# Forgetting attention in a hybrid encoder layer: one PSUM bank moved from the transposed scores to the side products

## The chip, the cores and the metric

The kernel runs on one core of a Trainium2 chip. Five engines work from queues of their own: TensorE (PE; its weight loads are PEld), VectorE (DVE), ScalarE (ACT), GpSimd (POOL) and SyncE (SP), which here issues the transfers. The metric is the device time of one execution in microseconds; lower is better. All times of the trace are microseconds from the start of its span.

## What is computed

One layer of a streaming encoder on 1024 tokens of width 1024, in float32: `h = x + W_out [FoX ++ GLA]`, then cross attention to 256 memory tokens, then a squared-ReLU MLP. The part that matters is the forgetting attention (FoX) with 8 heads of width 64, and the memory's keys and values, which do not depend on it:

```python
# forgetting attention, per head; c = cumulative sum of the log forget gates
s = einsum('bqhd,bkhd->bhqk', qb, kb) * scale
s = where(k_pos <= q_pos, s + c[q] - c[k], -inf)
out = einsum('bhqk,bkhd->bqhd', softmax(s), vb)
# memory side of the cross attention
k, v = split(rms_norm(mem) @ wkv, 2)
k = rms_norm(k)
# output projection of both mixers
h = x + concat([fox_out, gla_out]) @ w_out
```

## The kernel before

Matmul operands are split into a high and a low part (fp32r), and `gemm` (lines 103 to 110) makes three matmuls for each 128 rows of the sum: high x high, low x high, high x low. `evac_split` (112) takes a finished PSUM tile out in two instructions: ACT copies it (the high part), then DVE subtracts that copy from the tile (the low part). A PSUM tile of 128 x 512 floats is called a bank here.

`mixer_inputs` makes the projections, the gated linear attention (GLA) and, at its end, the values of FoX. It opens FoX (`fox_open`, 593) and starts the first group of scores before the values are done.

`fox` (646) loops over 8 heads and, in each head, over 2 groups. `fox_group` makes the scores of four blocks of 128 queries. `fox_scores` (617) does each: matmuls of queries and keys (628, 629) and a mask (631) into a score tile, the negated maximum on DVE (633), the exponential with its sum on ACT (636), the reciprocal on DVE (638), and the scaling on POOL (639). `values` (655) then takes two query blocks: for each pair of key blocks it transposes the probabilities on PE (666, 668) into a bank `tr`, takes it out with `evac_split` (671), and multiplies with the values into `pv` (675, 676). Line 678 (ACT) and line 681 (DVE) take `pv` out into `mixf`. A head has four calls of `values`, with 1, 2, 3 and 4 such `tr` tiles: 80 in all.

After each call of `values`, `step` (688) runs a piece of `side_work` (705), which is meant to lie beside the attention. It consists of the GLA half of the output projection for the first 512 columns (`out_part`, 758, 8 products of 12 matmuls), the keys and values of the memory (731 to 754, 8 products of 24 matmuls), and the second 512 columns with the GLA half and the first four FoX heads (8 products of 18 matmuls). Each product fills one bank `mm`. `out_part` takes it out with one DVE addition (776), the memory's keys with an ACT copy (744), its values with `evac_split` (738). The keys are also transposed, through a bank of `tr` (749 to 752), into a tile `mkv` that exists once and is emptied by a store (753).

The PSUM pools while FoX runs:

| pool | tiles | banks |
|---|---|---|
| `mm2` (651) | `mm`, the side products | 1 |
| `pv2` (652) | `pv` | 1 |
| `tr2` (653) | `tr`, transposed scores and memory keys | 3 |
| `sps` (596) | `s1` (one bank), `s2` (two banks), the scores | 3 |

That makes eight. After FoX, the next projection (`project_out`, 808) opens `mm3` with 2 banks, `tr3` with 2 (225, 226) and `mm3b` with 4 (812). It adds the rest of the FoX heads: its first operands are splits of `mixf` (`split_half`, 794), one for each pair of heads.

The order of the instructions on each engine is not written by hand. The Tile framework plans it at build time (`schedule_with_timeline_sim=True`, 1311) from the program order and its own estimate of each duration: an instruction takes its place when its operands and its buffer are free by that estimate. On the chip each engine runs its queue in that fixed order, and waits where an operand or a buffer is late. A pool that lands on the bytes of closed pools waits for every user of them, unless it is opened with `reuse_waits="tile"`, which these are not.

Of the kernel before, what the change touches and what calls it, by code (L numbers as in the profile page):

```python
# [24 lines left out]
PSUM = bass.MemoryType.PSUM  # L25
# [22 lines left out]
def f(ap):  # L48
    return ap.bitcast(F32)


class Layer:
# [593 lines left out]
    def fox(self):  # L646
        nc = self.nc
        with ExitStack() as st:
            pt = self.open(st, "foxpt", 5)
            olp = self.open(st, "foxol", 3)  # L650
            mmp = self.open(st, "mm2", 1, space=PSUM)
            pvp = self.open(st, "pv2", 1, space=PSUM)
            trp = self.open(st, "tr2", 3, space=PSUM)

            def values(h, sb, pp, A):
                va = A[4]
                pv = self.T(pvp, [P, 256], F32, "pv")
                nb = 2 * sb + 2
                for b in range(sb + 1):
                    tp = self.T(trp, [P, 512], F32, "tr")  # L660
                    for j in range(2):
                        kb = 2 * b + j
                        for i in range(2):
                            o = tp[:, j * 256 + i * P:j * 256 + (i + 1) * P]
                            if kb > 2 * sb + i:
                                nc.tensor.matmul(o, self.zerob, self.zerob, start=True, stop=True)
                            else:
                                nc.tensor.transpose(o, pp[i][:, kb * P:(kb + 1) * P], self.ident)  # L668
                    th = self.T(pt, [P, 512], F32R, "pth")
                    tl = self.T(pt, [P, 512], F32R, "ptl")  # L670
                    self.evac_split(th, tl, tp)
                    for j in range(2):
                        kb = 2 * b + j
                        js = slice(j * 256, (j + 1) * 256)
                        nc.tensor.matmul(pv, va[:, kb, :], th[:, js], start=kb == 0, stop=False)  # L675
                        nc.tensor.matmul(pv, va[:, kb, :], tl[:, js], start=False, stop=kb == nb - 1)  # L676
                ol = self.T(olp, [64, 256], F32, "ol")
                nc.scalar.activation(ol, pv[64:128, :], AF.Copy)
                o = self.mixf[(h % 2) * 64:(h % 2) * 64 + 64, 2 * sb:2 * sb + 2, h // 2, :]
                v3 = lambda ap: ap.rearrange("p (a b) -> p a b", a=2)  # L680
                nc.vector.tensor_tensor(o, v3(pv[0:64, :]), v3(ol), ALU.add)

            side = self.side_work(self.side, mmp, trp)
            prep = self.fox_prep
            next(side)
            A = self.fox_first

            def step(s):
                for _ in range(((s + 1) * 30 + 8) // 32 - (s * 30 + 8) // 32):
                    next(side, None)  # L690

            for h in range(8):
                nc.sync.dma_start(f(A[4]), self.vd[:, h])
                for g in range(2):
                    pp = self.fox_group(h, g, A) if h + g else self.fox_p
                    if g == 0 and h < 7:
                        An = prep(h + 1)
                    for sb in (g, g + 2):
                        values(h, sb, (pp[2 * sb], pp[2 * sb + 1]), A)
                        step(4 * h + 2 * g + sb // 2)  # L700
                A = An
            for _ in side:
                pass
# [611 lines left out]
```

## Time and profile before

| | |
|---|---|
| median of 3 runs | 1467.38 us (1467.37 to 1469.64) |
| the profiled execution as a whole | 1473.37 us |
| its span, first to last instruction | 1471.6 us |
| mean granted TensorE clock | 0.989 |
| FoX with side work, after the values' projection | 335 to 577 us of the span |

A row of the view by stretch gives the stretch, its length, and for each engine the busy time with the number of instructions, then the granted TensorE clock as a share of full speed, the busy share of the DMA engines and GB/s. A row of the view of waits gives the engine and line that stood idle, what released it, the total, the number of times and the longest. A row of the timeline gives start, duration, engine, line, operation, the tiles written and read, the shape, how many equal instructions are merged, and in square brackets an idle time just before with its releaser. Matmuls are pipelined: the duration of one is longer than the distance to the next.

### The profile page before, as it was taken

How to read it: one execution, taken by the hardware profiler on the slowest of the kernel's cores; microseconds unless marked ns; L12 is line 12 of the kernel's file. 1: busy time of each engine (PE TensorE's matmuls, PEld its weight loads, DVE VectorE, ACT ScalarE, POOL GpSimd, SP SyncE). 2: the span in 40 equal slices, each digit the busy share in tenths (PEclk: the TensorE clock that was granted, in tenths of full speed). 3: DMA queues.
4: the chain of work that ended last, by engine and by line, in shares of the span. 5: the costliest groups of instructions: out<-in, count | busy, mean ns of one | idle time of the engine just before them, and what ended most of it. 6: DMA issues, size and time to landing. Idle time of an engine off the chain costs nothing.

```text
span 1471.6 us, 19266 instructions
## 1 busy us (share of the span) xinstructions
PE 1435.6 (98%) x7068; PEld 1198.2 (81%) x7068; DVE 934.8 (64%) x1328; ACT 685.1 (47%) x1095; POOL 431.7 (29%) x456
## 2 busy tenths in 40 slices
PE   9999999999998999999999999999999999999998
PEld 7777888887877787888888878887888878888887
DVE  5387412427776676656654885645556958788797
ACT  4464322326776555445442254545445736334230
POOL 4146503324473311621212200000000532333454
PEclk9999999999999999999999999999999999999999
DMA  7425620268576742414375124444445846337353
GB/s 273 124 47 129 153 74 4 72 159 266 181 205 197 194 156 70 144 38 136 115 243 214 44 72 172 172 172 162 169 160 212 313 132 210 126 110 231 108 205 122
DMA packets 121166, 223.94 MB, mean 152 GB/s; under 512 B 8912, under 2 KB 54512, under 8 KB 118512
## 3 DMA queue, kind: packets, MB, share of 16 engines
q1 hardware_dynamic: 119776, 218.25, 45.9%
q10 hardware_dynamic: 1296, 4.46, 1.0%
q8 instruction: 56, 0.92, 0.3%
q14 instruction: 38, 0.31, 0.1%
HBM read 150.59 MB, written 72.09 MB: 151 GB/s over the span
## 4 chain that ended last, share of the span: by engine, by line
PE 82%; DMA 7%; DVE 4%; ACT 3%; issue 2%; POOL 1%; SPq 0%; DVEq 0%; ACTq 0%
PE mm L108 14%; PE mm L109 14%; PE mm L110 13%; PE my L109 7%; PE my L110 7%; PE my L108 7%; PE tr L109 3%; PE tr L108 3%; PE tr L110 3%; PE tr L668 2%; DMA xt<-in_x_dram 1%; DMA raw<-in_w_in_dram 1%; PE pv L675 1%; PE pv L676 1%; PE s L628 1%
## 5 line engine op out<-in xcount | busy, mean ns | idle before, releaser
L108 PE MATMUL my<-x,g 128*128 128x512 f32 x464 | 180.8, 390 | 1.5 <-ACT h L1251 1.5
L109 PE MATMUL my<-x,g 128*128 128x512 f32 x464 | 180.9, 390 | 1.3 <-DVE x L1046 1.3
L110 PE MATMUL my<-x,g 128*128 128x512 f32 x464 | 180.7, 390 | 0.0
L108 PE MATMUL mm<-wh,xh 128*128 128x512 f32 x320 | 128.7, 403 | 0.3 <-ACT wh L97 0.3
L109 PE MATMUL mm<-wl,xh 128*128 128x512 f32 x320 | 127.7, 399 | 0.0
L110 PE MATMUL mm<-wh,xl 128*128 128x512 f32 x320 | 127.4, 398 | 0.0
L1045 ACT ACTIVATE g<-s 128x1024 fp32r<-128x1024 f32 (+1 forms) x72 | 68.9, 963 | 103.9 <-PE my L110 37.6
L1046 DVE TENSOR_TENSOR g<-raw,g 128x512 fp32r<-128x512 f32 (+3 forms) x72 | 67.9, 946 | 69.2 <-ACT g L1045 69.1
L1071 POOL TENSOR_TENSOR s<-raw 128x384 f32<-128x384 f32 (+1 forms) x20 | 25.6, 1279 | 282.9 <-issue 217.0
L108 PEld LDWEIGHTS my<-x,g 128*128 128x128 f32 x464 | 87.2, 188 | 19.9 <-ACT h L1251 1.9
L109 PEld LDWEIGHTS my<-x,g 128*128 128x128 f32 x464 | 87.2, 188 | 19.6 <-DVE x L1046 1.7
L1045 ACT ACTIVATE g<-raw 128x512 fp32r<-128x512 f32 (+3 forms) x72 | 55.5, 773 | 101.8 <-DMA raw<-in_mlp_w_dram 39.9
L110 PEld LDWEIGHTS my<-x,g 128*128 128x128 f32 x464 | 87.2, 188 | 18.0
L1046 DVE TENSOR_TENSOR g<-s,g 128x1024 fp32r<-128x1024 f32 (+1 forms) x72 | 88.7, 1236 | 7.2 <-ACT g L1045 7.2
L639 POOL TENSOR_SCALAR p<-p,rrec 128x128 f32<-128x128 f32 (+3 forms) x64 | 50.6, 792 | 126.6 <-DVE rrec L638 117.0
L1213 DVE TENSOR_TENSOR x<-x 128x1024 fp32r<-128x1024 f32 (+1 forms) x64 | 77.1, 1226 | 15.7 <-ACT x L1212 15.7
L108 PE MATMUL mm<-x,g 128*128 128x512 f32 x220 | 85.9, 390 | 0.0
L110 PE MATMUL mm<-x,g 128*128 128x512 f32 x220 | 85.8, 390 | 0.0
L109 PE MATMUL mm<-x,g 128*128 128x512 f32 x220 | 85.7, 390 | 0.0
L108 PE MATMUL tr<-x,g 128*128 128x512 f32 x212 | 82.6, 389 | 0.0
L110 PE MATMUL tr<-x,g 128*128 128x512 f32 x212 | 82.6, 389 | 0.0
L109 PE MATMUL tr<-x,g 128*128 128x512 f32 x212 | 82.6, 389 | 0.0
(319 smaller groups left out, 3787.3 us busy)
## 6 DMA issues: line engine op xcount, KB each, us to landing
ud<-h SPq DMA_DIRECT2D x32, 768.0 KB
x<-ud SPq DMA_DIRECT2D x48, 512.0 KB
raw<-in_mlp_w_dram SPq DMA_DIRECT2D x20, 1024.0 KB
raw<-in_mlp_w_dram SPq DMA_DIRECT2D x16, 768.0 KB
raw<-in_w_in_dram SPq DMA_DIRECT2D x23, 512.0 KB
raw<-in_xattn_wkv_dram SPq DMA_DIRECT2D x16, 512.0 KB
od<-o SPq DMA_DIRECT2D x32, 256.0 KB
ud<-h SPq DMA_DIRECT2D x32, 256.0 KB
```

What stands on the lines that cost most here:

```text
L108: mm(ps, lh[k], rh[k], start=start and k == 0, stop=False, **kw)
L109: mm(ps, lh[k], rl[k], start=False, stop=False, **kw)
L110: mm(ps, ll[k], rh[k], start=False, stop=stop and k == n - 1, **kw)
L628: nc.tensor.matmul(ps[:, c], qa[:, ts], ka[:, c], start=True, stop=False)
L639: nc.gpsimd.tensor_scalar(p[:, 0:n], p[:, 0:n], rr, 1.0, ALU.mult, ALU.mult)
L668: nc.tensor.transpose(o, pp[i][:, kb * P:(kb + 1) * P], self.ident)
L675: nc.tensor.matmul(pv, va[:, kb, :], th[:, js], start=kb == 0, stop=False)
L676: nc.tensor.matmul(pv, va[:, kb, :], tl[:, js], start=False, stop=kb == nb - 1)
L1045: self.nc.scalar.activation(hi, src, AF.Copy)
L1046: self.nc.vector.tensor_tensor(lo, src, f(hi), ALU.subtract)
L1071: eng.tensor_tensor(s[:, 0], raw[:, 3], raw[:, 2], ALU.add)
L1213: nc.vector.tensor_tensor(lo, f(lo), f(hi), ALU.subtract)
```

## The change

```diff
@@ fox
             pt = self.open(st, "foxpt", 5)
             olp = self.open(st, "foxol", 3)
-            mmp = self.open(st, "mm2", 1, space=PSUM)
+            mmp = self.open(st, "mm2", 2, space=PSUM)
             pvp = self.open(st, "pv2", 1, space=PSUM)
-            trp = self.open(st, "tr2", 3, space=PSUM)
+            trp = self.open(st, "tr2", 2, space=PSUM)
```

The side products get two banks in place of one, and the transposes (of the scores and of the memory's keys) two in place of three. The sum stays at eight. No computation changes; the planner makes a new order with the new pools.

## The prediction

> **What bounds the kernel now.** I read the page first, for the whole run.
>
> ```profile
> span 1471.6 us, 19266 instructions
> PE 1435.6 (98%) x7068; PEld 1198.2 (81%) x7068; DVE 934.8 (64%) x1328; ACT 685.1 (47%) x1095; POOL 431.7 (29%) x456
> ```
>
> TensorE (PE) is busy 98% of the span, so a change of buffers gains where PE stands idle or runs slowly, and nowhere else. Next I read the busy time by stretch: the end of the mixer's projections, the forgetting attention while it has side products, its tail without them, and the projection after it.
>
> ```profile
> core 0: us, PE busy (x) PEld busy (x) DVE busy (x) ACT busy (x) POOL busy (x), PEclk, DMA share, GB/s
> 300.00:335.00 35.00, 35.00 (x174) 29.08 (x173) 8.28 (x15) 10.94 (x21) 9.18 (x13) 1.00 0.68 175
> 335.00:549.50 214.50, 203.47 (x1183) 172.01 (x1182) 151.19 (x279) 137.27 (x292) 90.83 (x115) 0.97 0.68 201
> 549.50:577.10 27.60, 22.25 (x146) 19.52 (x145) 22.88 (x46) 19.83 (x42) 5.98 (x8) 0.88 0.16 48
> 577.10:620.00 42.90, 42.90 (x196) 35.60 (x195) 26.23 (x35) 18.34 (x29) 22.28 (x18) 1.00 0.43 135
> ```
>
> Both neighbours have a full PE at clock 1.00. The attention does not: PE idles 214.50 - 203.47 = 11.0 us in the body and 27.60 - 22.25 = 5.4 us in the tail, and the granted clock is 0.97 and 0.88 there, worth another 0.03 x 214.5 = 6.4 and 0.12 x 27.6 = 3.3 us. So 26 us at most lie in the stage that the change touches. What ends PE's idle times there, in the answer on waits for 335 to 577 us:
>
> ```profile
> PE mm L108 <- DVE mkv L119: 4.0, 2, 3.0
> PE tr L668 <- DVE mkv L116: 2.9, 1, 2.9
> PE mm L108 <- DVE t2k L776: 1.9, 1, 1.9
> PE pv L676 <- DVE ptl L116: 1.8, 1, 1.8
> PE tr L668 <- DVE ptl L116: 1.6, 1, 1.6
> PE mm L108 <- ACT t2k L744: 0.7, 1, 0.7
> ```
>
> The columns are the total, the number of times and the longest. The three "mm" rows are a side product that stands before the evacuation of the product ahead of it, whose bank it needs: 4.0 + 1.9 + 0.7 = 6.6 us in four waits. The two "tr" rows are transposes that stand before an evacuated bank: 2.9 + 1.6 = 4.5 us in two waits. So the side bank is the dearer one now, but "tr" with its three banks already binds twice.
>
> **The change part by part.** No instruction is added or removed; on every engine the work is the same. What moves is which bank frees which instruction, and with it the planner's order.
>
> (a) The second side bank. The timeline of PE around one of the four waits:
>
> ```profile
> 338.52 0.39 PE L108 MATMUL mm<-sh,wh 128*128 128x512 f32 x1
> 338.75 0.40 PE L109 MATMUL mm<-sl,wh 128*128 128x512 f32 x1
> ...
> 344.31 0.80 PE L108 MATMUL mm<-sh,wh 128*128 128x512 f32 x1 [1.85 <-DVE t2k L776]
> 344.90 0.63 PE L109 MATMUL mm<-sl,wh 128*128 128x512 f32 x1
> ...
> 347.46 0.42 PE L109 MATMUL mm<-sl,wh 128*128 128x512 f32 x1
> ```
>
> Warm matmuls start 0.23 us apart (338.52, 338.75). After the wait, seven matmuls take from 344.31 to 347.46, 3.15 us in place of 7 x 0.23 = 1.61: the wait costs 1.54 us more than its own length, as slow clock. With a second bank this product needs no evacuation; it uses the same split operands as the one before, so they are there. The longest wait:
>
> ```profile
> 487.91 0.67 ACT L118 ACTIVATE mkv<-mm,mr 128x512 fp32r<-128x512 f32 x1
> 490.17 0.74 DVE L119 SCALAR_TENSOR_TENSOR mkv<-mm,mr,mkv 128x512 fp32r<-128x512 f32 x1
> 490.96 0.80 PE L108 MATMUL mm<-sh,wh 128*128 128x512 f32 x1 [3.00 <-DVE mkv L119]
> 494.11 0.47 PE L109 MATMUL mm<-sl,wh 128*128 128x512 f32 x1
> ```
>
> Here too 490.96 to 494.11 holds seven matmuls at 0.45 us, 1.54 us of slow clock. The other two waits (1.01 and 0.74 us) show none. Full gain: 6.6 + 2 x 1.54 = **9.7 us**. Lower bound of the gain is nothing: a PE that arrives earlier can meet the next late operand. Nearest to the rows is the full removal, which I take, and count what comes late next under (c).
>
> On the slow clock the Trainium skill, TensorE: Matmul & The Clock Gate, section "HAM oscillation — how this bites in real kernels", gives the rule that only idle gaps over about 3.4 us must be avoided. By that rule none of the four waits costs clock, and (a) would be 6.6 us in place of 9.7; the trace disagrees, with half speed after 1.85 us.
>
> (b) The tail gets filler. The program opens its PSUM pools one behind the other, so before the change the two banks of `mm3` (the next projection's) should lie on those of `mm2` and `pv2`, and wait for the last `pv`; after it they lie on the two of `mm2`, which are done when the side work is. What the tail has of transposes and of side products, and when the projection starts:
>
> ```profile
> 549.50:577.10 27.60, 9.61 (x55) 7.15 (x50) 10.53 (x16) 8.37 (x15) 0.88 0.16 48
> 549.50:577.10 27.60, 0.00 (x0) 0.02 (x1) 0.46 (x1) 0.00 (x0) 0.88 0.16 48
> ...
> 548.20 0.62 ACT L802 ACTIVATE sh<-mixf 128x512 fp32r<-128x512 f32 x1
> 550.68 0.68 DVE L803 TENSOR_TENSOR sl<-mixf,sh 128x512 fp32r<-128x512 f32 x1
> 577.19 0.40 PE L108 MATMUL mm<-sh,wh 128*128 128x512 f32 x1
> ```
>
> The first row is `tr`'s instructions (55 on PE, 16 DVE evacuations), the second `mm`'s: no product runs in the tail, although three of the four operand pairs of the next projection are split by 551.4. Two free banks let 2 x 9 matmuls run early, 18 x 0.23 = 4.1 us, into 5.4 us of idle time. Bounds: 0 and 4.1 us. I take **2 us**, since the idle time lies in pieces of 0.2 to 1.9 us and attention work goes first.
>
> (c) The third transposing bank is lost. How long one is held, at the shortest and where the tail is dense:
>
> ```profile
> 336.45 0.41 PE L668 MATMUL tr<-ident,p 128*128 128x128 f32 x2
> ...
> 574.00 0.38 PE L668 MATMUL tr<-ident,p 128*128 128x128 f32 x2
> 575.23 0.69 DVE L116 TENSOR_TENSOR ptl<-tr,pth 128x512 fp32r<-128x512 f32 x1
> 552.83 1.06 PE L668 MATMUL tr<-ident,p 128*128 128x128 f32 x4
> 555.60 0.67 DVE L116 TENSOR_TENSOR ptl<-tr,pth 128x512 fp32r<-128x512 f32 x1
> ```
>
> From the first transpose to the end of the DVE subtraction: 575.92 - 574.00 = 1.9 us, and 556.27 - 552.83 = 3.4 us. In the tail, 16 tiles at 3.4 us need 3.4/2 - 3.4/3 = 0.57 us each more with two banks than with three: 9 us at most, if the banks alone set the pace; at the shortest hold, two banks give one tile per 0.96 us, well under the 27.60/16 = 1.7 us that the tail takes per tile now, and cost nothing. I take **2 us**, nearer to nothing, because scores and `pv` products of other tiles can go between. In the body side products cover the gaps, and by the list of first transposes and evacuations in the timeline (336.45 to 574.00, 84 tiles) 37 of the 84 opened while two others were held, 28 of them in the body. The price is what the planner's order misses. Bounds: nothing; and, if these 37 fail as often as the 24 side products (8 + 8 + 8 by the loops) on one bank do now (four in 24, 6.6/4 = 1.65 us each), six waits, 10 us, of which half followed by 1.54 us of slow clock: 14.6 us. Three banks show two such waits, 4.5 us; I take as much again, **4.5 us**.
>
> (d) The tile of the side work that shares `tr`. Its hold, in the chain that ended last:
>
> ```profile
> 442.32 6.63 DMA kTd<-mkv
> 449.04 0.61 ACT mkv L115
> 449.67 0.70 DVE mkv L116
> 450.41 1.12 PE tr L668 x4
> ```
>
> One bank is held until the store that empties `mkv` has landed, and PE waits 2.92 us behind it. With two banks only one would be left for the attention during that store's 6.6 us. This happens at worst four times (four such tiles); it is inside the bounds of (c), and not added.
>
> Sum: -9.7 - 2 + 2 + 4.5 = **-5.2 us**. The profiled execution took 1473.37 us as a whole (span 1471.6), 6.0 us over the median of 1467.38; I put the difference on the median: 1462.2 us.
>
> **The rivals.** Rival 1, the wait only moves: PE is in order, and DVE is busy 151 of 214.5 us and ACT 137. A PE that is no longer stopped at a side product comes sooner to an evacuation that is as late as before. Then (a) is eaten by new `tr` and `pv` waits, and the time is 1466 to 1468, say 1467. For it: the late evacuations (487.91 on ACT, 490.17 on DVE) are late through queueing, which no bank shortens. Against: one full bank of lead is 12 to 24 matmuls, 2.8 to 5.5 us, more than any of the four waits. A sentence in the Trainium skill, TensorE: Matmul & The Clock Gate, section "HAM oscillation — how this bites in real kernels", tells of a kernel in which PSUM double-buffering gave no further gain; by it, rival 1. No run here shows that kernel.
>
> Rival 2, slower: the third transposing bank was the one that let PE run ahead. At the upper bound of (c), with (a) in full and nothing of (b): -9.7 + 14.6 + 2 = +6.9, so 1474.3 us. It decides when more than four of the 37 tight tiles become waits with slow clock behind (9.7 / 2.4 each, 1.65 + half of 1.54).
>
> Rival 3, the change doesn't do what it says: the next side product lacks its weights or split operands, and the second bank stays empty. Then (a) and (b) are nothing: +4.5 + 2, 1473.9 us. The operands speak against it for the waits at 344 and 490; the weights arrive late at times.
>
> **How the numbers follow.** Forecast case (net gain of 3 to 14 us) 0.47; rival 1 within 2.9 us of no change 0.24; rival 2 0.24; rival 3 0.05. A measurement of this kernel tells about 0.2%, 2.9 us, from no change. So faster 0.47, same 0.24, slower 0.29. Low end: -9.7 - 4.1, nothing under (c): 1453.6. High end: between rival 2 and its addition of the tail's bound of 9 us in place of 2, short of the very end: 1476. The forecast case alone is 1453.5 to 1464.5.
>
> **What would show it.** Right: no PE wait on `mkv L119` or `t2k` before an `mm`; a clock of 0.99 or more in the body; `mm` matmuls inside the tail; the time from the first transpose to the last `pv` shorter by 5 us. Wrong: `tr L668` waits on `ptl L116` of over 8 us in total, or a tail of over 31 us. If the stage is shorter but the end is not, a later transfer took it.

## The result, and the profile after

The kernel after takes 1476.87 us (median of 7 runs, 1470.77 to 1479.58), the kernel before beside it 1468.7 us (7 runs, 1467.37 to 1471.48). The ratio is 1.0051, with a 95% interval of 1.0035 to 1.0067: slower by about 7.5 us, on the other side of no change than the forecast of 1462.2, and 0.9 us above the upper end of its range. In what follows a ratio is turned into microseconds with the 1468 us of before.

The head of the page of the kernel after:

```profile
span 1474.9 us, 19255 instructions
PE 1437.8 (97%) x7068; PEld 1196.2 (81%) x7068; DVE 934.6 (63%) x1328; ACT 684.5 (46%) x1095; POOL 429.1 (29%) x456
```

The same 7068 matmuls, in a longer span. The two profiled executions differ by 1474.9 - 1471.6 = 3.3 us only, since that of before lay 4.7 us above its median and that of after 0.3 us below its own. The traces shown here carry less than half of the difference of the medians.

The view by stretch of the kernel before: the stage from the first transpose to the last `pv`, first the heads 0 to 6, then the last head (columns as before: length, busy time and count of PE, PEld, DVE, ACT, POOL, clock, DMA share, GB/s).

```profile
336.40:557.40 221.00, 207.90 (x1209) 176.26 (x1208) 157.77 (x292) 141.59 (x303) 91.85 (x116) 0.96 0.68 200
557.40:577.10 19.70, 16.43 (x112) 14.48 (x113) 14.98 (x31) 14.11 (x29) 4.80 (x6) 0.91 0.00 1
```

The same of the kernel after, with the whole stage ahead of its two parts, then, in the same view for the side bank's instructions alone, the last 42 us of it:

```profile
336.20:586.30 250.10, 231.15 (x1342) 192.63 (x1341) 174.19 (x322) 154.90 (x330) 94.09 (x122) 0.98 0.59 177
336.20:567.00 230.80, 214.72 (x1237) 179.66 (x1236) 160.32 (x296) 141.43 (x302) 89.83 (x117) 0.98 0.64 191
567.00:586.30 19.30, 16.43 (x108) 12.97 (x107) 13.87 (x26) 13.48 (x28) 4.26 (x5) 1.00 0.00 1
```

```profile
544.70:586.30 41.60, 6.43 (x24) 4.24 (x24) 0.68 (x1) 0.00 (x0) 1.00 0.15 45
```

The stage went from 240.7 to 250.1 us. The last row says that 24 matmuls of the next projection now stand inside it (there were none), 24 x 0.23 = 5.5 us of work that is no longer behind it; without them it is 244.6, 3.9 us longer than before. PE's idle time in it went from 240.7 - 224.3 = 16.4 to 250.1 - 231.15 = 19.0 us, although the wait on the side bank is gone. The waits of PE in 335 to 586.3 us of the kernel after, down to 0.7 us:

```profile
PE s L628 <- ACT p L636: 6.2, 7, 1.7
PE tr L668 <- DVE mkv L116: 3.3, 2, 2.4
PE pv L676 <- DVE ptl L116: 3.3, 8, 1.0
PE tr L668 <- DVE ptl L116: 2.4, 3, 1.1
PE pv L675 <- ACT wh L86: 1.9, 1, 1.9
PE tr L751 <- DVE mkv L116: 0.7, 1, 0.7
```

No side product stands before an evacuation any more: the 6.6 us of the three "mm" rows of before are gone. In their place score matmuls (line 628) wait for the exponential that empties their bank, 6.2 us in seven waits. In the kernel before that row was this, for 335 to 600 us:

```profile
PE s L628 <- ACT p L636: 1.3, 2, 1.0
```

The longest of the new waits and one more, in the timeline of ACT and PE:

```profile
396.35 1.15 ACT L86 ACTIVATE wh<-raw 128x512 fp32r<-128x512 f32 x2 [2.92 <-DMA raw<-in_xattn_wkv_dram]
...
397.40 0.35 ACT L636 ACTIVATE p<-s,nm 128x128 f32<-128x128 f32 x1
...
397.89 0.39 PE L628 MATMUL s<-ka,qa 128*128 128x256 f32 x1 [1.66 <-ACT p L636]
...
399.05 0.42 PE L108 MATMUL mm<-wh,sh 128*128 128x512 f32 x1
...
399.29 0.61 PE L109 MATMUL mm<-wl,sh 128*128 128x512 f32 x1
...
399.70 0.63 PE L110 MATMUL mm<-wh,sl 128*128 128x512 f32 x1
...
402.48 0.39 PE L676 MATMUL pv<-ptl,va 128*128 128x256 f32 x1
...
405.84 0.63 ACT L86 ACTIVATE wh<-raw 128x512 fp32r<-128x512 f32 x1 [4.11 <-DMA raw<-in_xattn_wkv_dram]
406.38 0.46 ACT L636 ACTIVATE p<-s,nm 128x256 f32<-128x256 f32 x1
...
406.98 0.45 PE L628 MATMUL s<-ka,qa 128*128 128x384 f32 x1 [1.52 <-ACT p L636]
```

This is read from the top. ACT is in order, and in its queue the copy of a weight block for the side work (line 86) stands ahead of an exponential. The block has not landed, ACT stands 2.92 us, the exponential of 0.35 us starts at 397.40, and PE, whose next scores need that bank, has been idle for 1.66 us. At 405.84 the same happens once more. From 399.29 to 402.48 seven matmuls of 512 columns and one of 256 take 3.19 us; at the warm distances of 0.23 and 0.12 us they would take 1.73, so 1.46 us more are lost as slow clock. The view by stretch has the granted clock at 0.50 there:

```profile
399.30:402.50 3.20, 3.20 (x10) 2.54 (x9) 3.01 (x6) 1.94 (x5) 0.91 (x2) 0.50 1.06 160
```

Three stretches of heads, from transposes that stand at the same place of the program: of the kernel before heads 1, 3 and 5 to 6, then the same of the kernel after.

```profile
362.60:394.30 31.70, 31.44 (x187) 26.18 (x185) 26.47 (x52) 22.41 (x50) 11.00 (x18) 1.00 0.71 218
422.20:453.30 31.10, 27.33 (x174) 23.49 (x173) 22.85 (x45) 21.80 (x49) 19.65 (x24) 0.95 0.77 227
486.10:557.40 71.30, 66.23 (x377) 56.32 (x375) 50.40 (x90) 41.46 (x87) 18.73 (x23) 0.95 0.56 170
```

```profile
371.40:412.90 41.50, 38.32 (x210) 32.00 (x208) 27.90 (x50) 28.28 (x59) 22.85 (x31) 0.96 0.59 155
437.60:469.10 31.50, 25.41 (x153) 20.93 (x152) 22.66 (x42) 20.89 (x45) 17.35 (x22) 0.95 0.76 226
509.60:567.00 57.40, 55.06 (x336) 46.61 (x334) 42.23 (x81) 35.30 (x76) 11.80 (x16) 1.00 0.51 152
```

The gain is where it was forecast, late in the stage: in heads 5 and 6 the idle time falls from 5.1 to 2.3 us and the clock goes from 0.95 to 1.00. The loss is earlier: head 3 is idle for 6.1 in place of 3.8 us, with fewer side products left for it (24 matmuls in place of 38, since others ran ahead), and head 1, which holds the two waits shown above, is idle for 3.2 us at a clock of 0.96, where before it was idle for 0.3 us at 1.00.

### The profile page after: what moved, and what is told of

Its sections match the earlier page's. It is cut to its first block, busy times and chain, and to the rows that moved or that the text cites. A ratio compares the mean times of both kernels' runs of the same rounds, so it can differ in the third digit from the quotient of the medians.

```text
span 1474.9 us, 19255 instructions
## 1 busy us (share of the span) xinstructions
PE 1437.8 (97%) x7068; PEld 1196.2 (81%) x7068; DVE 934.6 (63%) x1328; ACT 684.5 (46%) x1095; POOL 429.1 (29%) x456
## 4 chain that ended last, share of the span: by engine, by line
PE 61%; DMA 4%; DVE 3%; issue 2%; ACT 2%; POOL 1%; DVEq 0%; SPq 0%; ACTq 0%; POOLq 0%
PE mm L108 8%; PE mm L110 8%; PE mm L109 8%; PE my L109 7%; PE my L110 7%; PE my L108 7%; PE tr L108 3%; PE tr L110 3%; PE tr L109 3%; PE tr L668 1%; DMA qa<-qd 1%; PE s L628 1%; PE pv L676 1%; DMA raw<-in_mlp_w_dram 1%; ACT p L636 1%
## 5 line engine op out<-in xcount | busy, mean ns | idle before, releaser
L109 PEld LDWEIGHTS my<-x,g 128*128 128x128 f32 x464 | 87.1, 188 | 19.7 <-DVE x L1046 1.7
L1213 DVE TENSOR_TENSOR x<-x 128x1024 fp32r<-128x1024 f32 (+1 forms) x64 | 77.3, 1228 | 15.1 <-ACT x L1212 14.6
L639 POOL TENSOR_SCALAR p<-p,rrec 128x128 f32<-128x128 f32 (+3 forms) x64 | 47.6, 753 | 126.2 <-DVE rrec L638 126.1
```

The lines of the kernel that those rows point to most:

```text
L109: mm(ps, lh[k], rl[k], start=False, stop=False, **kw)
L639: nc.gpsimd.tensor_scalar(p[:, 0:n], p[:, 0:n], rr, 1.0, ALU.mult, ALU.mult)
L1213: nc.vector.tensor_tensor(lo, f(lo), f(hi), ALU.subtract)
```

## The experiments

All were timed in five rounds against the kernel before on the same chip; since the chips of the groups differ, two runs are compared by their ratios. The letters of the theories are those of the expectations, each of which says what its letter stands for.

| run | kernel | median us | ratio to before, 95% | us |
|---|---|---|---|---|
| e1_tr2_only | one side bank, two transposing banks | 1487.02 | 1.0128, 1.0103 to 1.0153 | +18.8 |
| e5_tr2_held | the same, eighth bank held | 1487.07 | 1.0134, 1.0113 to 1.0156 | +19.7 |
| r3_tr2_off4 | e1 at offset 4 | 1489.72 | 1.0141, 1.0121 to 1.0160 | +20.7 |
| r4_tr2_off12 | e1 at offset 12 | 1489.23 | 1.0142, 1.0119 to 1.0164 | +20.8 |
| e2_after_gate1 | after, side work one call ahead at most | 1485.45 | 1.0113, 1.0094 to 1.0131 | +16.6 |
| e7_after_gate4 | after, four calls ahead at most | 1489.09 | 1.0137, 1.0121 to 1.0154 | +20.1 |
| e3_before_gate1 | before, one call ahead at most | 1481.35 | 1.0089, 1.0072 to 1.0106 | +13.1 |
| e4_pv_first | after, next projection kept out | 1478.56 | 1.0072, 1.0050 to 1.0093 | +10.6 |
| e6_after_keys_in_mm | after, memory keys by a side bank | 1473.49 | 1.0030, 1.0013 to 1.0047 | +4.4 |
| e8_before_mkv2 | before, `mkv` twice | 1472.41 | 1.0021, 1.0009 to 1.0034 | +3.1 |
| n1_before_off4 | before at offset 4 | 1470.95 | 1.0016, 1.0005 to 1.0027 | +2.3 |
| n2_before_off12 | before at offset 12 | 1467.80 | 0.9996, 0.9985 to 1.0007 | -0.6 |
| n3_after_off4 | after at offset 4 | 1469.81 | 1.0002, 0.9990 to 1.0015 | +0.3 |
| n4_after_off12 | after at offset 12 | 1475.15 | 1.0044, 1.0028 to 1.0060 | +6.5 |
| r1_after_raw3 | after, three raw buffers | 1467.68 | 1.0004, 0.9990 to 1.0017 | +0.6 |
| r2_before_raw3 | before, three raw buffers | 1466.21 | 0.9984, 0.9971 to 0.9998 | -2.3 |
| s1_after_raw3_off12 | r1 at offset 12 | 1469.65 | 1.0015, 1.0002 to 1.0029 | +2.2 |
| s2_raw3_keys | r1 with e6's edit | 1473.52 | 1.0038, 1.0024 to 1.0051 | +5.6 |

### The lost transposing bank alone

In the kernel before only line 653 is changed; the second kernel, besides, holds the bank that this leaves over, so that nothing can use it.

```diff
-            trp = self.open(st, "tr2", 3, space=PSUM)
+            trp = self.open(st, "tr2", 2, space=PSUM)
```

```diff
+            pad = self.T(self.open(st, "pad2", 1, space=PSUM), [P, 512], F32, "pad")
...
+            nc.vector.tensor_copy(pad[64:128, 0:1], self.mixf[64:128, NT - 1, 3, 0:1])
```

> One side bank as before the change, two transposing banks as after it; the eighth bank stays unused. Theory A (the side products run ahead of the attention through their second bank, use up the filler and leave PE without it at 428 to 472 us): the loss needs the second side bank, so this kernel stays within 3 us of before (1466 to 1472 us), with the side products at most 5 calls of values ahead. Theory B (the third transposing bank is what was needed): slower than before by 6 us or more (1474 us or over), with PE waits of tr L668 on ptl L116 of over 5 us in total.

> One side bank, two transposing banks, and the eighth bank held by an unused tile that one copy of a single column touches after the last attention output, so that the next projection finds its banks as in the kernel before. Theory B (the third transposing bank is what the attention needs): as slow as the run with the bank left free, 1483 to 1490 us. Theory C (a third of that run's 18 us came from the next projection, which was planned early on the free bank and then waited for its residuals): 1476 to 1482 us, with the stage from the last pv to the last sum of that projection back at the 37 us of the kernel before.

Both cost about 19 us. Held or free, the eighth bank makes no difference, so it is the lost bank itself, the term (c) of the forecast, at 18.8 us where 6.5 were put down. Theory B has its time, and not its sign: the waits of `tr` on `ptl` in 335 to 600 us of e1_tr2_only are 3.8 us and not over 5. The stage of e1_tr2_only by stretch (heads 0 to 6, then the last head), the side bank's instructions in the last head alone, and the first rows of PE's waits in the first part:

```profile
336.60:572.20 235.60, 215.59 (x1221) 179.64 (x1220) 162.12 (x296) 141.62 (x303) 92.75 (x117) 0.96 0.63 188
572.20:596.60 24.40, 22.14 (x137) 18.46 (x136) 13.87 (x26) 13.32 (x28) 4.29 (x5) 1.00 0.00 1
```

```profile
572.20:596.60 24.40, 9.21 (x36) 6.41 (x36) 0.00 (x0) 0.00 (x0) 1.00 0.00 1
```

```profile
PE s L628 <- ACT p L636: 4.1, 3, 2.5
PE pv L675 <- DVE mixf L681: 3.1, 2, 2.1
PE tr L668 <- DVE ptl L116: 2.7, 2, 1.5
PE mm L108 <- DVE mkv L119: 2.7, 1, 2.7
PE mm L108 <- DVE t2k L776: 2.4, 2, 1.9
```

The part with side work grew from 221.0 to 235.6 us, 14.6 us, for 1221 PE instructions in place of 1209; the last head, less the 36 matmuls of the next projection (8.3 us), shrank from 19.7 to 16.1 with eleven instructions fewer. In e5_tr2_held, where nothing of the next projection can lie in the stage, the same two parts are:

```profile
332.10:569.30 237.20, 216.96 (x1221) 180.87 (x1221) 161.48 (x296) 141.50 (x304) 92.66 (x117) 0.95 0.64 187
569.30:588.70 19.40, 15.41 (x101) 11.88 (x100) 13.87 (x26) 13.38 (x28) 4.26 (x5) 1.00 0.00 1
```

The body grew by 16.2 us, and the last head is as long as before. So within the stage the price lies in the body, none in the tail. A part falls behind the stage: from the last `pv` to its last sum the next projection takes 37.2 us in the kernel before, 35.0 in e1_tr2_only, although 8.3 us of its matmuls lie ahead of it (PE waits there 0.9, 1.4 and 1.4 us), and 40.0 in e5_tr2_held.

No row of the waits names the price. The row that a missing bank should raise, "tr" on `ptl`, has 2.7 us in the body. The body's idle time rose from 13.1 to 20.0 us through small rows of other kinds (scores on exponentials 4.1 us, where before had 1.3 in all; `pv` on `mixf` 3.1, where the body before has no such row). The other 7.7 us are busy time of PE, for twelve instructions more and at the same granted clock of 0.96, so slow clock is not the price. The `pv` products alone are busy 50.30 us (274 of them) in place of 41.92 (264); how much of that is lost time isn't settled.

One sum over PE's timeline does show the bank. The idle time that stands directly behind a transpose, whatever the next instruction waits for, is 3.5 us in the body of the kernel before, 14.7 in e1_tr2_only and 14.8 in e5_tr2_held (15.5 and 14.4 in r3_tr2_off4 and r4_tr2_off12, against 5.0 and 3.7 in the kernel before at the same offsets). Behind all other instructions it fell from 9.6 to 5.3 us in e1_tr2_only. With two banks the planner lays the matmuls in another order, and in that order PE makes its transposes and then stands before whatever comes next.

The second side bank, which the change gives for it, is worth the difference of e1_tr2_only and the change: 18.8 - 7.5 = 11.3 us.

### Does PE run too far ahead with side products?

The second bank lets up to eight calls' worth of side products stand ahead in the order, and later stretches of the attention then have none beside them. The gate ties the side products to the end of an earlier call of `values`; the same gate stands in the kernel before as a control, and a wider one (`len(done) - 5`) in the kernel after.

```diff
+                        last = nc.tensor.matmul(pv, va[:, kb, :], tl[:, js], start=False, stop=kb == nb - 1)
...
+                done.append(last.ins)
...
-                    next(side, None)
+                    with self.tc.issue_after(done[max(len(done) - 2, 0)]):
+                        next(side, None)
```

> The changed kernel, and each side product's instructions on PE queued behind the last pv matmul of the call of values before the one that it follows in the program, so that no product runs more than one call ahead (up to 8 in the changed kernel). Theory A: the drought of side products at 428 to 472 us goes, and the time falls by 6 us or more, to 1470 us or less, with no stretch of over 20 us without side products before the last of them. Theory B: nothing of the transposes' banks is changed, so 1474 us or more.

> The kernel before with the same queueing of the side products: the control. Theory A: running ahead by 4 to 5 calls, as the kernel before does at 388 to 432 us, is a small part of the same loss, so same or up to 4 us faster than before (1464 to 1469 us). Theory B makes no difference here (1466 to 1471 us). Slower by over 3 us would say that the queueing itself costs, through side products that wait behind a late pv.

> The changed kernel with the side products queued on PE behind the pv of four calls of values earlier, so that they run at most four calls ahead in place of eight. Theory A in a milder form (only the long lead does harm): faster than the changed kernel by 3 us or more, 1474 us or less. If running ahead is a gain throughout, as the runs with a lead of one say: slower than the changed kernel or the same, 1476 to 1484 us.

All three are slower than without a gate. In e7_after_gate4 PE waits most where the change already hurt:

```profile
PE s L628 <- ACT p L636: 19.3, 7, 6.6
```

Held back, PE stands at the score banks instead. The control was to show whether the gate costs something by itself, and at 13.1 us it does, so the gated kernels can't tell what running ahead costs. What refutes theory A as the main cause is e1_tr2_only: it has no second side bank, and it loses more than the change.

### The next projection in the tail, and the memory's keys

`e4_pv_first` opens `pv2` ahead of `mm2`, so that the next projection's banks wait for the last `pv` again. `e6_after_keys_in_mm` transposes the memory's keys in a side bank (line 749). `e8_before_mkv2` gives the kernel before a second `mkv` tile.

```diff
-            mmp = self.open(st, "mm2", 2, space=PSUM)
             pvp = self.open(st, "pv2", 1, space=PSUM)
+            mmp = self.open(st, "mm2", 2, space=PSUM)
```

```diff
-                tp = self.T(trp, [P, 512], F32, "tr")
+                tp = self.T(mmp, [P, 512], F32, "mm")
```

```diff
-                kv = self.T(mp, [P, 2, 512], F32R, "mkv")
+                kv = self.T(mp, [P, 2, 512], F32R, "mkv", bufs=2)
```

> The changed kernel with pv2 opened ahead of mm2, so that the two banks of mm3 lie on pv2 and one of mm2 and have to wait for the last pv. If the 24 matmuls of the next projection that lie ahead of the last pv in the changed kernel were worth their 24 x 0.23 = 5.5 us, this is slower than the changed kernel by 3 to 6 us (1479 to 1483 us), with no such matmul ahead of the last pv. If the tail's idle time costs nothing more, within 2 us of the changed kernel.

> The changed kernel with the four transposed tiles of the memory's keys in a side bank in place of a transposing bank. If the price of the two transposing banks is these four holds (one bank kept until the store of the tile before has landed), the PE waits on mkv L116 before tr L668 go and the time falls by 4 us or more, to 1473 us or less. If the price is in the tiles of the attention itself, within 3 us of the changed kernel (1474 to 1480 us).

> The kernel before with two tiles mkv in place of one, so that no evacuation waits for a store of the memory's keys or values. The waits on mkv in the kernel before are 2.9 us before tr L668 and 4.0 us before mm L108, with slow clock behind them: if they are what they seem, 3 to 8 us faster than before (1461 to 1466 us). If the waits only move, within 3 us of before.

Without the 24 matmuls in the tail the kernel is 1.7 us slower by the medians (1478.56 to 1476.87) and 3.1 by the ratios; the two intervals overlap, so (b)'s 2 us fit and are not proved. Keys in the side bank won 3.1 us by the ratios, less than the 4 us that would have made them the price, and took the waits of `tr` on `mkv` away; here too the intervals overlap. The second `mkv` won nothing; the wait of `tr` on `mkv` and one of the two of `mm` went, and others came at the scores (5.8 us of line 628 on line 636).

### Is it the order that was planned?

The offset 8 in line 689 sets after which calls the side work pauses (the 5th and the 21st). At 4 it is the 3rd and 19th, at 12 the 7th and 23rd. The work is the same, the planned order another.

```diff
-                for _ in range(((s + 1) * 30 + 8) // 32 - (s * 30 + 8) // 32):
+                for _ in range(((s + 1) * 30 + 4) // 32 - (s * 30 + 4) // 32):
```

> The kernel before with the 30 pieces of side work spread over the 32 calls of values with an offset of 4 in place of 8, so that the two calls without a piece are the 3rd and the 19th in place of the 5th and the 21st. The work and the banks are the same; the planner makes another order (some hundreds of lines of PE's queue differ). Theory E (the order before is a lucky one, and any new order costs some us): 1473 us or more. Theory B (the loss is the third transposing bank): within 3 us of before (1466 to 1472 us).

> The same with an offset of 12 (the 7th and the 23rd call without a piece). Theory E: 1473 us or more. Theory B: 1466 to 1472 us.

> The changed kernel with an offset of 4. Theory E: anywhere between before and 1490 us, and on the mean of the three offsets no slower than the three of the kernel before. Theory B: slower than the kernel before with the same offset by 5 to 12 us.

> The changed kernel with an offset of 12. Theory E: as for the offset of 4. Theory B: slower than the kernel before with the same offset by 5 to 12 us.

> The transposing bank lost without the second side bank (one side bank, two transposing banks, the eighth bank unused), with the offset of the steps at 4 in place of 8. If the price of the lost bank is of the chain itself, it stands at every offset: the ratio is 1.010 to 1.015 as at offset 8 (1.0128). If it depends on the planned order as the change's own price does (7.7 us at offset 8, none at 4), the ratio is 1.004 to 1.008.

> The same kernel (one side bank, two transposing banks, the eighth bank unused) with the offset of the steps at 12. Price of the chain itself: ratio 1.010 to 1.015. Price of the order: it differs from those of offsets 4 and 8 by over 0.004 in either direction.

The kernel before lies within 3 us at all three offsets, so as far as three orders show it was no lucky one. The lost bank alone costs 18.8, 20.7 and 20.8 us against the kernel before at offset 8, or 18.8, 18.4 and 21.4 against that of the same offset: that price stands over the orders. But what the second side bank gives back does not: the change as a whole, each against the kernel before at its own offset, costs 7.5 us at 8, 0.3 - 2.3 = -2.0 at 4, and 6.5 + 0.6 = 7.1 at 12 (each difference is uncertain by 2 to 3 us). Theory B, which had the change slower by 5 to 12 us at both new offsets, is right at 12 and fails at 4.

### Are late weight blocks behind the rest?

The blocks of weights come through two `raw` buffers (line 213). A third lets the next load start while the two before it are still in use.

```diff
-            self.rawp = self.open(ws, "raw", 2)
+            self.rawp = self.open(ws, "raw", 3)
```

> The changed kernel with a third buffer for the raw weight blocks (2 to 3), so that the loads of the memory's weights are issued a block earlier and ScalarE's in-order weight copies (line 86) need not stand for them. Theory F (the price of the changed order is ScalarE standing behind late weight loads, with the attention's exponentials behind it): the idle time of line 86 before the blocks of in_xattn_wkv_dram falls from 18.1 us (335 to 600 us) to under 6, the score matmuls' waits for the exponentials (line 628) from 6.2 to under 2, and the ratio to before from 1.0051 to 1.0015 or less (1470 to 1471 us). Theory G (the lost bank for transposes is paid inside the chain of transposes and values, whatever ScalarE waits for): the weight waits fall, the ratio stays at 1.004 to 1.006 (1475 to 1478 us), and the transposes and values matmuls wait for the probabilities' tiles more.

> The control of the run before it: the kernel before with a third raw buffer. Theory F: it has 9.8 us of waits for blocks of in_xattn_wkv_dram, of which score matmuls wait for little, so 0 to -2 us (ratio 0.9985 to 1.0). If it gains as much as the changed kernel does (5 us or more), the buffer is worth that by itself and says nothing of the change. Theory G: no difference here, ratio 0.999 to 1.001.

> The changed kernel with the third raw buffer at the offset of the steps where the change cost as much as at 8 (offset 12: ratio 1.0044 with two raw buffers). Theory F (late weight blocks are where the change's price comes from, at every offset): ratio 0.999 to 1.0015, 4 to 8 us under the same kernel with two buffers. Theory H (the third buffer only drew another order at offset 8, as offset 4 did): the ratio may lie anywhere from 1.000 to 1.006, and one of 1.003 or more speaks for it.

> The changed kernel with the third raw buffer and, besides, the transposes of the memory's keys in the side bank instead of a bank for the transposes (line 749). It is to beat both kernels if the keys' 3.4 us, which were measured with two raw buffers, stand beside those of the third: ratio 0.997 to 0.999 (1464 to 1467 us). If the two edits take away the same waits, it stays at 1.000 to 1.001, as with the third buffer alone.

ACT's waits for the memory's weights in 335 to 600 us, with PE's waits at the scores, of the kernel after and of r1_after_raw3:

```profile
ACT wh L86 <- DMA raw<-in_xattn_wkv_dram: 18.1, 9, 4.1
PE s L628 <- ACT p L636: 6.2, 7, 1.7
```

```profile
ACT wh L86 <- DMA raw<-in_xattn_wkv_dram: 6.7, 2, 3.6
PE s L628 <- ACT p L636: 3.7, 4, 2.2
```

Head 1 of r1_after_raw3, to be read against 371.40:412.90 of the kernel after, and its head 3:

```profile
365.60:403.00 37.40, 37.40 (x220) 31.88 (x219) 28.70 (x51) 25.94 (x56) 23.54 (x29) 1.00 0.61 177
430.00:464.00 34.00, 27.64 (x154) 22.45 (x153) 22.46 (x42) 20.78 (x45) 17.30 (x22) 0.90 0.72 208
```

Head 1 runs with a full PE at clock 1.00, and takes 37.4 in place of 41.5 us with ten PE instructions more. That is the place where the kernel after had its weight blocks late. Head 3 is as poor as in the kernel after, 6.4 us idle at a clock of 0.90. By the ratios the third buffer is worth 6.9 us to the changed kernel and 2.3 us to the one before, so the change costs 0.6 + 2.3 = 2.9 us (uncertain by 2.8) with it in place of 7.5. At offset 12 it takes the changed kernel from 6.5 to 2.2 us. These 4.3 us are at the low end of what theory F expected, and theory H, by which the buffer only draws another order, allows them too: the two aren't separated. The score waits fell to 3.7 and not below 2; and n3_after_off4, which pays no price, has 16.1 us of the same ACT waits, n1_before_off4 17.7. So the total isn't what counts; which of the waits an exponential stands behind may be. In s2_raw3_keys the keys' edit, which won 3.1 us with two buffers, costs 5.0 us with three: it is no cost of its own, and an effect of that size from one edit may be a matter of the order that it draws. What in s2_raw3_keys costs the 5 us isn't settled; its waits for weights are short too (6.3 us).

## Why the prediction was wrong

- **What bounds the kernel.** Right: the stage is the only one that moved, and the projection behind it has a full PE at clock 1.00 in both.
- **The signs.** Of those for a right forecast two came (no `mm` waits for the evacuation of the product ahead, `mm` matmuls lie in the tail) and two did not: the clock is 0.98 in the heads 0 to 6, and the stage is longer by 9.4 us in place of shorter by 5.
- **(a), 9.7 us by the second side bank.** The mechanism was right: all "mm" waits on evacuations are gone, and the last heads run at clock 1.00. With (b) the forecast was 11.7 us. The experiments give 11.3 us at offset 8, by e1_tr2_only less the change; the same difference is 20.7 - 0.3 = 20.4 us at offset 4 and 20.8 - 6.5 = 14.3 at 12. Held against e5_tr2_held, in which the next projection can't start early either, it is 19.7 - 7.5 = 12.2 us at offset 8. The size wasn't too large. Slow clock had a place in the sum (behind a wait of 1.66 us another 1.46 were lost), though the last section has a wait of the same length as one of the two counted, with none behind it.
- **(b), 2 us.** Right in kind: 24 matmuls of the next projection (18 were put down) now lie ahead of the last `pv`. e4_pv_first puts it at 1.7 to 3.1 us, unresolved.
- **(c), 6.5 us by the lost transposing bank: the step that failed.** It was sized at 4.5 us in the body and 2 in the tail, by analogy with the rows of waits on `tr`; four kernels without the third bank measure 18.8 to 20.8 us. The tail's part was nothing. The body's part is 14.6 us in e1_tr2_only and 16.2 in e5_tr2_held, at and over the upper bound of 14.6 us that the text named for it and passed over for a value near the low end. That the bound was met is luck: it was added up from six waits of transposes and slow clock behind half of them, and neither is what grew. Up to 6 us more fell in the projection behind the stage, for which (c) had no term. The error was to look for the price in one row: the text said "The price is what the planner's order misses", and then counted only waits of transposes. The row that was to show it wrong, `tr` on `ptl` over 8 us, stood at 2.4; the bank was paid where PE stands behind its transposes (3.5 us before, 14.7 without the bank), before scores and `pv` products, and in busy time at the same clock.
- **(d)** lay inside (c). The waits of `tr` on `mkv` went from 2.9 to 3.3 us: no larger price of its own was seen, and e6_after_keys_in_mm, without these holds, won 3.1 us, unresolved.
- **Rival 1**, the wait only moves: in part. New waits at the scores (4.9 us more) stand against the 6.6 that went, but the second bank is worth 11 us or more. The sentence that the prediction takes from the Trainium skill, TensorE: Matmul & The Clock Gate, section "HAM oscillation — how this bites in real kernels", that PSUM double-buffering gave no further gain, is of another kernel and doesn't carry over to this one.
- **Rival 2**, the third bank let PE run ahead: it named what decided, the third bank, and its 1474.3 us is nearest. That it came near is in part luck, since both of its terms were too small: it had 9.7 against 14.6 + 2, and the runs have 11.3 against 18.8.
- **Rival 3**: refuted, the second bank is in use.
- **What neither named:** ACT in order behind late weight blocks. The forecast said that no instruction is added, and priced no queue but PE's. At offset 8 about 4.6 us of the 7.5 go away with a third raw buffer (7.5 - 2.9), most visibly in head 1; whether by the blocks or by the new order that comes with the buffer isn't separated.

What stays open: why PE's busy time grew by 7.7 us beside the 6.9 us of idle time in the body of e1_tr2_only; and why one edit moves the kernel by 3 to 5 us in either direction. Of the kernels run, the kernel before with three raw buffers is the fastest, 2.3 us under the kernel before, with an interval that ends at 0.9998; the change with three raw buffers doesn't beat it.

## What to carry to other kernels

A bank taken from a chain of several engines (transpose, copy, subtract, multiply) is priced by running the kernel without that bank, not by the rows of waits on it: here they said 4.5 us, and the loss was about 19, spread over rows of other names and a longer busy time. Before giving a bank to one kind of product, look at what a PE that runs ahead will ask of the queues beside it: here weight copies came to stand ahead of exponentials on ACT, and with one more load buffer, and the order that came with it, 4.6 of the 7.5 us were gone. Where a planner makes the order, measure the change at two or three neighbouring orders before believing a difference of 5 us.

## What the runs showed that was not expected

Slow clock can come late: after the wait of 1.66 us that ended at 397.89 the next matmuls started 0.23 us apart, and only from 399.29, 1.4 us on, they started about 0.42 apart, until 402.48. In the kernel before (the waits at 344 and 490 us) it began with the wait's end. By the rule that the prediction takes from the Trainium skill, TensorE: Matmul & The Clock Gate, section "HAM oscillation — how this bites in real kernels", only idle gaps over about 3.4 us must be avoided; this trace disagrees again, after a wait of 1.66 us.

Nor is slow clock sure to come. In n2_before_off12 the first side product waits as long as in the kernel before, 1.85 us, and the clock stays full, where the wait at 344 us was followed by matmuls at half speed:

```profile
340.86 0.50 PE L108 MATMUL mm<-sh,wh 128*128 128x512 f32 x1 [1.85 <-DVE t2k L776]
```

```profile
340.90:344.40 3.50, 3.50 (x20) 2.92 (x20) 3.50 (x6) 1.53 (x4) 1.59 (x3) 1.00 1.01 346
```

A term for slow clock that is read from one trace is therefore less sure than the wait itself.

The granted clock of the stage is 0.96 in the trace of the kernel before and 0.98 in that of the kernel after, and the stage is longer all the same: the clock of a stretch is no measure of its loss unless the idle time is read beside it.
